# Feed-forward input products of a two-layer decoder trunk: seven half-size products in place of eight, three weight sums by adding transfers, Silu in place of tanh

## The chip, the core and the metric

The kernel runs on one core of a Trainium2 chip. A core has five engines that work side by side, each through a queue of its own in program order: TensorE (PE, with its weight loads shown apart as PEld), VectorE (DVE), ScalarE (ACT), GpSimd (POOL) and SyncE (SP, which here only issues transfers). Sixteen DMA engines move data. The metric is device microseconds of one execution; before the change the median of three runs is 1450.72 us (1449.16 to 1450.77).

## The reference, cut to what matters

512 tokens of width 1024 go through two layers. Each layer has a mixer (attention with a forget gate and a short convolution in layer 0, a gated linear recurrence in layer 1), a cross-attention into 256 memory rows, and a feed-forward block; each of the three adds its normalised output to the residual stream. All data are float32. The change concerns the first half of the feed-forward block:

```python
D_FF = ((8 * D_MODEL // 3 + 255) // 256) * 256          # 2816
def swiglu(h, w_gu, w_down):
    g, u = jnp.split(h @ w_gu, 2, axis=-1)
    return (jax.nn.silu(g) * u) @ w_down
...
        h = rmsnorm(x, g_ffn_pre[layer])
        y = swiglu(h, w_ffn_gu[layer], w_ffn_down[layer])
        x = x + rmsnorm(y, g_ffn_post[layer])
```

`h @ w_gu` is a product of 512x1024 by 1024x5632, twice in the kernel (once a layer).

## The kernel before

**Numbers.** A float32 operand is split into two parts of 12 significant bits, high and low, and a product is high by high plus low by high plus high by low, three matmuls into one float32 sum in PSUM (`mm3`, L276 to L279). So every weight that comes in is split: ACT casts it to the high part (L354, `wh`), DVE subtracts that from the raw value for the low part (L355, `wl`). `split_out` does both.

**Feed-forward, first half** (`ffn`, L634 on). The weights come in chunks of 256 columns and all 1024 rows, as two transfers of 512 KB on SP's queue (`load_raw`, L117) into buffers called `st`, of which there are four; the split parts go into four `wh` and four `wl` buffers. A chunk times the activations `hT` (features on partitions, four row tiles in each half of the features, 512 tokens) gives two blocks of 128 columns by 512 tokens, each in one PSUM bank. That is 2 blocks x 8 row tiles x 3 = 48 matmuls with 512 tokens as the moving side. There are 11 pairs of chunks (jp = 0 to 10), each one gate chunk and one up chunk. jp 0 is special (`ws_gemm_split`, L332): it runs the first 256 tokens and then the other 256, so that the norm of the last tokens can go on beside it. The other 10 pairs are 20 plain chunk products in each layer, 40 in all; the text calls each of them a chunk. Then `act` makes silu(gate) x up from the banks: a tanh on ACT, (tanh + 1) x gate on DVE, times up on DVE, twice the wanted value; the factor of a half is put in when `parts` splits the result for the next product (L657 on).

**What is around it.** Ahead stands the cross-attention's output product (`OutProj.half1`, L418), which for each of four tiles of 128 tokens runs the residual and the next norm (`chain`, `next`; one small power on POOL at L210 for each of the two norms) and the transposes that fill `hT` (`put_T`, L258, with copies out of PSUM by ACT at L268 and DVE at L269). Behind it stands the feed-forward's second product, `OutProj.run` with `w_ffn_down`; its left side is made by `parts`, two row tiles at a time.

**What sets the order.** PE's instructions stand in the order in which the program writes them. The other engines' instructions are put in order by a scheduler when the program is built; on the chip each engine then takes its queue strictly in that order, and an instruction that waits holds up all that stand behind it. A buffer of a pool (`st`, `wh`, `wl`, the 14 large groups, the 8 small `s` tiles, 4 + 4 PSUM banks) is used again as soon as its last reader is done, and the transfer or write that takes it waits for that reader.

Of the kernel before, what the change touches and what calls it, by code (L numbers as in the profile page):

```python
# [15 lines left out]
P = 128  # L16
# [26 lines left out]
def trunk_kernel(ctx: ExitStack, tc: tile.TileContext, a: dict, out: bass.AP):  # L43
    """Residual stream x stays on chip, tokens on partitions. Each sub-layer's input is normalised,
    transposed (features on partitions) and split exactly into two float32r parts of 12 significant
    bits; weights are split the same way. A float32 product is then high*high + low*high + high*low
    in the float32 accumulators of PSUM."""
# [54 lines left out]
    def load_gain(ap, engine=nc.scalar):  # L102
        """A gain spread over the partitions, as two halves of the features."""
# [50 lines left out]
    def log1p(e, w, s):  # L154
        """log(1 + e) for e in [0, 1], as 2 artanh(e / (2 + e)); e is overwritten by the result."""
# [18 lines left out]
    def setup_chan():  # L174
# [8 lines left out]
        # lamc = -8 softplus(-lam), lamh = half of it  # L183
# [16 lines left out]
    def rstd(st):  # L200
        """st[:, 0:2] sums of squares of the halves -> st[:, 4:5] = (mean + eps) ** -0.5"""
# [14 lines left out]
    def row_stats(xt, both=False):  # L216
        """(mean of squares + eps) ** -0.5 of the rows of one tile"""
# [12 lines left out]
    def scaled(xt, g, r):  # L230
        """Both halves of the normalised rows of one tile, tokens on partitions."""
# [13 lines left out]
    class Feat:  # L245
        """Activations with features on partitions: tile k's high and low parts."""
# [4 lines left out]
    def new_hT():  # L251
# [3 lines left out]
        ft.ghi, ft.glo = hi, lo  # L255
        return ft

    def put_T(hT, t, hs, bank=bankB):  # L258
        for hf in range(2):
# [6 lines left out]
            sl = slice(t * P, (t + 1) * P)  # L266
            last = (
# [13 lines left out]
    def w_chunk(w, c0):  # L281
        """256 columns of w, all rows: two pieces of four row tiles."""
# [815 lines left out]
```

## Time and profile before

| What | Before |
|---|---|
| runs | 1449.16, 1450.72, 1450.77 us |
| span of the profiled execution | 1447.4 us, 3.3 us under the median of the runs |
| PE busy, matmuls | 1437.3 us (99%), 7124 |
| DVE busy | 769.6 us (53%) |
| ACT busy | 567.8 us (39%) |
| POOL busy | 37.6 us (3%) |
| transfers | 151.03 MB, 104 GB/s over the span |
| the 20 chunks of layer 0 | from 419.24 us to 636.87 us, 217.6 us |
| the 20 chunks of layer 1 | from 1103.53 us to 1321.16 us, 217.6 us |

A page of the profile has the busy time of each engine, the span in 40 slices, the transfer queues, the chain of work that ended last, and the costliest groups of instructions by line. In a group's row stand the line, engine, operation, out<-in by the program's names and the shape, then busy time, the mean of one in ns, and the idle time of the engine ahead of it with what ended it. Matmuls overlap in the pipeline, so the mean of one matmul is longer than the distance between the starts of two; the distance is what counts and is read from the timeline. The profiled execution is one run; its span leaves out what lies ahead of the first and behind the last instruction.

### The profile page before, as it was taken

The numbers are of one execution on the slowest core, as the hardware profiler recorded it, in microseconds if no ns is written. First come the engines' busy times: TensorE is split into PE (matmuls) and PEld (weight loads), VectorE is DVE, ScalarE is ACT, GpSimd is POOL, SyncE is SP. The second block draws the span as 40 slices with busy tenths as digits, with TensorE's granted clock in tenths as the row PEclk, the third lists the DMA queues.
The fourth block names the chain that finished last, engine by engine and source line by source line (L and its number), as shares of the span: only waits on it lengthen the run. The fifth ranks groups of instructions, "written<-read, shape, count | busy, mean of one in ns | idle before, by whom it ended". The sixth has DMA issues, their size and how long they took to land.

```text
span 1447.4 us, 17847 instructions
## 1 busy us (share of the span) xinstructions
PE 1437.3 (99%) x7124; PEld 1208.5 (83%) x7124; DVE 769.6 (53%) x1171; ACT 567.8 (39%) x922; POOL 37.6 (3%) x82
## 2 busy tenths in 40 slices
PE   8999999999999999999999999999999999999998
PEld 6777789888898888888889888988889888888886
DVE  5785767544743333362447998754484333336232
ACT  4354455433532222252334786443362222225130
POOL 1000001000100000000000000000010000000000
PEclk9999999999999999999999999999999999999999
DMA  5633253520433323323513226352032323323321
GB/s 175 187 95 87 78 174 97 177 80 30 124 97 100 102 89 101 102 88 102 166 46 93 90 88 211 108 162 74 29 117 88 102 88 102 101 88 102 96 79 58
DMA packets 119373, 151.03 MB, mean 104 GB/s; under 512 B 6181, under 2 KB 88177, under 8 KB 119290
## 3 DMA queue, kind: packets, MB, share of 16 engines
q1 hardware_dynamic: 114722, 140.92, 31.3%
q10 hardware_dynamic: 3896, 6.86, 1.7%
q0 software_dynamic: 672, 2.11, 0.5%
q8 instruction: 56, 0.92, 0.3%
q14 instruction: 27, 0.22, 0.1%
HBM read 147.76 MB, written 2.11 MB: 104 GB/s over the span
## 4 chain that ended last, share of the span: by engine, by line
PE 98%; DMA 1%; DVE 0%; issue 0%; POOL 0%; SPq 0%; ACT 0%; DVEq 0%; POOLq 0%; ACTq 0%
PE bA L277 19%; PE bA L279 19%; PE bA L278 19%; PE bA L378 5%; PE bA L380 5%; PE bB L378 5%; PE bB L380 5%; PE bA L379 5%; PE bB L379 5%; PE bA L703 1%; PE bB L262 1%; PE bB L277 1%; PE bA L544 1%; PE bA L546 1%; PE bB L278 1%; PE bB L279 1%
## 5 line engine op out<-in xcount | busy, mean ns | idle before, releaser
L355 DVE TENSOR_TENSOR wl<-st,wh 128x1024 fp32r<-128x1024 f32 x228 | 278.6, 1223 | 402.9 <-ACT wh L354 401.7
L277 PE MATMUL bA<-hTh,wh 128*128 128x512 f32 (+1 forms) x1216 | 456.9, 376 | 0.0
L279 PE MATMUL bA<-hTh,wl 128*128 128x512 f32 (+1 forms) x1216 | 453.2, 373 | 0.0
L278 PE MATMUL bA<-hTl,wh 128*128 128x512 f32 (+1 forms) x1216 | 452.9, 372 | 0.0
L354 ACT CAST wh<-st 128x1024 fp32r<-128x1024 f32 x228 | 239.9, 1052 | 514.0 <-PE bA L278 359.7
L279 PEld LDWEIGHTS bA<-hTh,wl 128*128 128x128 f32 x1216 | 229.0, 188 | 40.3
L278 PEld LDWEIGHTS bA<-hTl,wh 128*128 128x128 f32 x1216 | 229.2, 189 | 38.6
L277 PEld LDWEIGHTS bA<-hTh,wh 128*128 128x128 f32 x1216 | 229.1, 188 | 38.5
L378 PE MATMUL bB<-wh,y 128*128 128x512 f32 x208 | 80.9, 389 | 0.0
L379 PE MATMUL bB<-wl,y 128*128 128x512 f32 x208 | 80.9, 389 | 0.0
L380 PE MATMUL bB<-wh,y 128*128 128x512 f32 x208 | 80.9, 389 | 0.0
L378 PE MATMUL bA<-wh,y 128*128 128x512 f32 x144 | 56.5, 392 | 0.0
L656 DVE TENSOR_TENSOR y<-sw,bA 128x512 f32<-128x512 f32 x44 | 30.2, 686 | 49.5 <-PE bA L279 49.3
L380 PE MATMUL bA<-wh,y 128*128 128x512 f32 x144 | 56.1, 390 | 0.0
L379 PE MATMUL bA<-wl,y 128*128 128x512 f32 x144 | 56.1, 389 | 0.0
L653 DVE SCALAR_TENSOR_TENSOR sw<-sw,bA 128x512 f32<-128x512 f32 x44 | 30.1, 683 | 35.1 <-ACT sw L652 35.1
L380 PEld LDWEIGHTS bB<-wh,y 128*128 128x128 f32 x208 | 39.0, 188 | 8.1
L378 PEld LDWEIGHTS bB<-wh,y 128*128 128x128 f32 x208 | 39.0, 188 | 8.1
L379 PEld LDWEIGHTS bB<-wl,y 128*128 128x128 f32 x208 | 39.0, 188 | 8.1
L652 ACT ACTIVATE sw<-bA 128x512 f32<-128x512 f32 x44 | 26.1, 594 | 48.1 <-PE bA L279 48.1
L210 POOL TENSOR_TENSOR post<-post,nhalf 128x1 f32<-128x1 f32 x24 | 13.2, 548 | 1004.0 <-DVE post L206 1004.0
L236 DVE SCALAR_TENSOR_TENSOR h<-x,pre,gain 128x512 f32<-128x512 f32 x44 | 31.3, 748 | 14.2 <-POOL pre L210 13.5
(248 smaller groups left out, 2035.8 us busy)
## 6 DMA issues: line engine op xcount, KB each, us to landing
st<-in_w_ffn_gu_dram SPq DMA_DIRECT2D x88, 512.0 KB, 3.6
st<-in_w_ffn_down_dram SPq DMA_DIRECT2D x44, 512.0 KB, 3.8
st<-in_w_xkv_dram SPq DMA_DIRECT2D x32, 512.0 KB, 5.0
st<-in_ab_w_in_dram SPq DMA_DIRECT2D x24, 512.0 KB, 3.8
st<-in_w_xq_dram SPq DMA_DIRECT2D x16, 512.0 KB, 3.5
st<-in_w_xo_dram SPq DMA_DIRECT2D x16, 512.0 KB, 3.6
st<-in_c_w_in_dram SPq DMA_DIRECT2D x16, 512.0 KB, 3.9
st<-in_ab_w_out_dram SPq DMA_DIRECT2D x8, 512.0 KB, 3.7
```

The source lines that it names most:

```text
L236: nc.vector.scalar_tensor_tensor(out=h, in0=xt[:, sl], scalar=r, in1=g[hf], op0=ALU.mult, op1=ALU.mult)
L277: nc.tensor.matmul(out=ps, lhsT=wh, rhs=xh, start=first, stop=False)
L278: nc.tensor.matmul(out=ps, lhsT=wh, rhs=xl, start=False, stop=False)
L279: nc.tensor.matmul(out=ps, lhsT=wl, rhs=xh, start=False, stop=last)
L354: nc.scalar.copy(out=hi, in_=src)
L355: nc.vector.tensor_tensor(out=lo, in0=src, in1=f(hi), op=ALU.subtract)
L378: nc.tensor.matmul(out=ps, lhsT=yh, rhs=wh[:, kk, :], start=first, stop=False)
L379: nc.tensor.matmul(out=ps, lhsT=yh, rhs=wl[:, kk, :], start=False, stop=False)
L380: nc.tensor.matmul(out=ps, lhsT=yl, rhs=wh[:, kk, :], start=False, stop=last)
L652: nc.scalar.activation(out=s, in_=gb[m], func=AF.Tanh, scale=0.5)
L653: nc.vector.scalar_tensor_tensor(out=s, in0=s, scalar=1.0, in1=gb[m], op0=ALU.add, op1=ALU.mult)
L656: nc.vector.tensor_tensor(out=y2[jp // 2][:, jp % 2 * 2 + m, :], in0=s, in1=ub[m], op=ALU.mult)
```

## The change

**Activations.** While the transposes of the feed-forward's norm leave PSUM, ACT also copies the unsplit value into two more groups (`hT.raw`, one for each half of the features). Feature halves and token halves (early 256, late 256) make four blocks: a11, a12 (late tokens) and a21, a22 (early tokens). After jp 0, DVE makes four differences of them in place, and each is split into a new group (`wa`).

**Weights.** A chunk's two row halves and two column blocks make B11, B12, B21, B22. The sums that are needed are t1 = B11 + B12, t3 = B12 + B22, t2 = t1 + B22 and t4 = t1 + B21 + B22. A third `st` buffer `tt` is loaded with the upper rows again, and a transfer from POOL's queue with an add at its destination puts the lower rows on top; a second adding transfer puts B11 on top of B12 in `r0`. (In the words of the change these are three sums: two column blocks in the first, one in the second.) DVE then adds `t2` and the first block of `tt`. Four splits follow instead of two: `r0`, `t2` (half as large), `tt` and `r1`.

**Products.** A chunk is now 7 products of 4 row tiles x 3 matmuls with 256 tokens as the moving side, 84 matmuls, in the order a11 b11, s2 t2, n1 t1, n3 t3, a12 b21, a22 t4, n4 b22. Between them ACT copies the first product out of PSUM, and DVE combines the products: three operations of 256 columns (q, u, v) and then two of 256 and one of 512 columns into the result. The gate chunk uses the four banks of one PSUM pool and the up chunk the four of the other.

**Silu.** ACT computes Silu itself, so the DVE operation with (tanh + 1) is gone, and `parts` needs no factor of a half. For chunks jp 1 to 10 Silu and the product with up run on data that the combination has written to SBUF.

The lines that only lost a comment are left out of the diff.

```diff
     def new_hT():
...
-        ft.ghi, ft.glo = hi, lo
+        ft.ghi, ft.glo, ft.raw = hi, lo, None
         return ft
     def put_T(hT, t, hs, bank=bankB):
...
             sl = slice(t * P, (t + 1) * P)
+            if hT.raw:
+                nc.scalar.copy(out=hT.raw[hf][:, :, sl], in_=v)
             last = (
...
+    class Winograd:
+        def __init__(self, hT):
+            r0, r1 = hT.raw
+            e, l = slice(0, 256), slice(256, 512)
+            a21, a11, a22, a12 = r0[:, :, e], r0[:, :, l], r1[:, :, e], r1[:, :, l]
+            sub = lambda o, i0, i1: nc.vector.tensor_tensor(out=o, in0=i0, in1=i1, op=ALU.subtract)
+            self.parts = {}
+            sub(a22, a21, a22)
+            sub(a21, a21, a11)
+            sub(a11, a11, a22)
+            for name, raw in (("s2", a11), ("n1", a22), ("n3", a21)):
+                self.put(name, raw)
+            sub(a12, a12, a11)
+            self.put("n4", a12)
+            for name, hf, sl in (("a11", 0, l), ("a12", 1, l), ("a22", 1, e)):
+                self.parts[name] = hT.ghi[hf][:, :, sl], hT.glo[hf][:, :, sl]
+
+        def put(self, name, raw):
+            g = group("wa")
+            self.parts[name] = g[:, :, 0:256], g[:, :, 256:512]
+            split_out(raw, *self.parts[name])
+
+        def weights(self, w, c0):
+            r0, r1 = load_raw(w, 0, 4, c0, 256), load_raw(w, 4, 4, c0, 256)
+            one, two = slice(0, P), slice(P, 2 * P)
+            add = lambda o, i0, i1: nc.vector.tensor_tensor(out=o, in0=i0, in1=i1, op=ALU.add)
+            t2 = sbuf("t2").rearrange("p (k c) -> p k c", k=4)
+            rows = w.rearrange("(k p) n -> p k n", p=P)
+            tt = load_raw(w, 0, 4, c0, 256)
+            nc.gpsimd.dma_start(out=tt, in_=rows[:, 4:8, c0:c0 + 256], accum_op=ALU.add)
+            nc.gpsimd.dma_start(out=r0[:, :, two], in_=rows[:, 0:4, c0:c0 + P], accum_op=ALU.add)
+            add(t2, tt[:, :, two], r0[:, :, one])
+            add(tt[:, :, one], tt[:, :, one], tt[:, :, two])
+            w1, w2 = split_w(r0, 4, 256), split_w(t2, 4, P)
+            w3, w4 = split_w(tt, 4, 256), split_w(r1, 4, 256)
+            return {"b11": (w1, one), "t1": (w1, two), "t2": (w2, one), "t4": (w3, one),
+                    "t3": (w3, two), "b21": (w4, one), "b22": (w4, two)}
+
+        def gemm(self, w, c0, bank, out):
+            ws = self.weights(w, c0)
+            one, two = slice(0, 256), slice(256, 512)
+            bks = [bank() for _ in range(4)]
+            x, y = sbuf("wx"), sbuf("wy")
+            p1, q, v, u = x[:, one], x[:, two], y[:, one], y[:, two]
+            def product(ps, a, b):
+                (hi, lo), (wt, ms) = self.parts[a], ws[b]
+                for k in range(4):
+                    mm3(ps, wt[0][:, k, ms], wt[1][:, k, ms], hi[:, k, :], lo[:, k, :], k == 0, k == 3)
+                return ps
+            tt = lambda o, i0, i1, op: nc.vector.tensor_tensor(out=o, in0=i0, in1=i1, op=op)
+            ps = product(bks[0][:, one], "a11", "b11")
+            nc.scalar.copy(out=p1, in_=ps)
+            ps = product(bks[1][:, one], "s2", "t2")
+            tt(q, ps, p1, ALU.subtract)
+            ps = product(bks[2][:, one], "n1", "t1")
+            tt(u, ps, q, ALU.add)
+            ps = product(bks[0][:, two], "n3", "t3")
+            tt(v, ps, q, ALU.add)
+            p2 = product(bks[3][:, two], "a12", "b21")
+            p4 = product(bks[3][:, one], "a22", "t4")
+            out(0, slice(256, 512), p2, p1, ALU.add)
+            out(0, slice(0, 256), p4, v, ALU.subtract)
+            product(bks[2][:, two], "n4", "b22")
+            out(1, slice(0, 512), bks[2], y, ALU.add)
...
+        hTf.raw = [f(group("raw")) for _ in range(2)]
         proj.half1()
...
-                nc.scalar.activation(out=s, in_=gb[m], func=AF.Tanh, scale=0.5)
-                nc.vector.scalar_tensor_tensor(
-                    out=s, in0=s, scalar=1.0, in1=gb[m], op0=ALU.add, op1=ALU.mult
-                )
-                nc.vector.tensor_tensor(out=y2[jp // 2][:, jp % 2 * 2 + m, :], in0=s, in1=ub[m], op=ALU.mult)
+                nc.scalar.activation(out=s, in_=gb[m], func=AF.Silu)
+                nc.vector.tensor_tensor(out=y_[:, m, :], in0=s, in1=ub[m], op=ALU.mult)
+        def act_wino(jp, wino):
+            s = [sbuf("sw") for _ in range(2)]
+            def gate(m, sl, ps, sb, op):
+                nc.vector.tensor_tensor(out=s[m][:, sl], in0=ps, in1=sb, op=op)
+                if sl.start == 0:
+                    nc.scalar.activation(out=s[m], in_=s[m], func=AF.Silu)
+            def up(m, sl, ps, sb, op):
+                nc.vector.tensor_tensor(out=y_[:, m, sl], in0=ps, in1=sb, op=op)
+                if sl.start == 0:
+                    nc.vector.tensor_tensor(out=y_[:, m, :], in0=y_[:, m, :], in1=s[m], op=ALU.mult)
+            wino.gemm(w, jp * 256, bankB, gate)
+            y_ = y_rows(jp)
+            wino.gemm(w, FF + jp * 256, bankA, up)
...
-            split_out(src, yg[:, 0:2, :], yg[:, 2:4, :], 0.5)
+            split_out(src, yg[:, 0:2, :], yg[:, 2:4, :])
...
         gb, ub = ws_gemm_split(w, [0, FF], hT, prev.hook)
         act(0, gb, ub)
+        wino = Winograd(hT)
         for jp in range(1, NFF // 2):
-            gb = ws_gemm(w, jp * 256, hT)
-            ub = ws_gemm(w, FF + jp * 256, hT)
-            act(jp, gb, ub)
+            act_wino(jp, wino)
```

The scheduler places the new work as follows. First, DVE's queue in the middle of layer 0's chunks, of the changed kernel, from the end of one up chunk into the next gate chunk. (`bA_4528` is the bank that the last of the seven products fills; `sw` is Silu's result; `st_4632` is the next chunk's `tt`, `st_4627` its `r0`, `st_4629` its `r1`, so that `wl_4643`, `wl_4647` and `wl_4651` are the low parts of `t2`, `tt` and `r1`; `wx_4658` takes q, `st_4754` is the `r0` of the chunk after.)

```order
L749 TENSOR_TENSOR y2_4244<-y2_4244,sw_4371 128x512
L747 TENSOR_TENSOR y2_4244<-bA_4528,wy_4531 128x512
L384 TENSOR_TENSOR t2_4631<-st_4632,st_4627 128x512
L749 TENSOR_TENSOR y2_4244<-y2_4244,sw_4372 128x512
L384 TENSOR_TENSOR st_4632<-st_4632 128x4x128
L432 TENSOR_TENSOR wl_4643<-t2_4631,wh_4642 128x512
L432 TENSOR_TENSOR wl_4647<-st_4632,wh_4646 128x1024
L432 TENSOR_TENSOR wl_4651<-st_4629,wh_4650 128x1024
L412 TENSOR_TENSOR wx_4658<-bB_4655,wx_4658 128x256
L432 TENSOR_TENSOR wl_4766<-st_4754,wh_4765 128x1024
```

Before, at the same place, four splits and four operations on the activations served a pair of chunks:

```order
L355 TENSOR_TENSOR wl_4768<-st_4765,wh_4767 128x1024
L653 SCALAR_TENSOR_TENSOR sw_4757<-sw_4757,bA_4645 128x512
L355 TENSOR_TENSOR wl_4774<-st_4771,wh_4773 128x1024
L653 SCALAR_TENSOR_TENSOR sw_4761<-sw_4761,bA_4646 128x512
L355 TENSOR_TENSOR wl_4830<-st_4827,wh_4829 128x1024
L656 TENSOR_TENSOR y2_4624<-sw_4757,bA_4707 128x512
L656 TENSOR_TENSOR y2_4624<-sw_4761,bA_4708 128x512
```

So the operations that make a chunk's `t2`, `t2`'s low part and `tt`'s low part now stand behind the operation that reads the last product of the chunk before, and q stands behind the splits of `tt` and `r1`.

Second, SP's queue of the changed kernel at the same chunks, with the semaphores that each transfer waits for. (`DMAHW` are raised by SP's and ACT's transfers, `DMASW` by POOL's, `DVE` and `Activation` by those engines; in POOL's queue of the same kernel, below it, the row of `st_4504` raises `DMASW4`, that of `st_4499` `DMASW3`.)

```order
L119 DMA st_4499<-in_w_ffn_gu_dram 128x4x256 [waits DMAHW0_49,DVE_49]
L119 DMA st_4501<-in_w_ffn_gu_dram 128x4x256 [waits DMAHW2_49,DMASW1_49,DMAHW6_49,DVE_49,Activation_49]
L119 DMA st_4504<-in_w_ffn_gu_dram 128x4x256 [waits DMASW2_49,DVE_49]
L119 DMA st_4627<-in_w_ffn_gu_dram 128x4x256 [waits DMAHW3_49,DVE_49]
L119 DMA st_4629<-in_w_ffn_gu_dram 128x4x256 [waits DMAHW1_49,DMASW3_49,DMAHW5_49,DVE_49,Activation_49]
L119 DMA st_4632<-in_w_ffn_gu_dram 128x4x256 [waits DMASW4_49,DVE_49]
```

```order
L389 DMA st_4499<-in_w_ffn_gu_dram 128x4x128
L388 DMA st_4504<-in_w_ffn_gu_dram 128x4x256
L389 DMA st_4627<-in_w_ffn_gu_dram 128x4x128
L388 DMA st_4632<-in_w_ffn_gu_dram 128x4x256
```

Each chunk's `tt` is loaded into the buffer of the `tt` of the chunk before (`st_4632` waits for the add into `st_4504` and for DVE, the last to read it), while `r0` and `r1` turn over the three other buffers. POOL's queue then holds only the adding transfers, `r0`'s ahead of `tt`'s. Before the change POOL had no work here, and SP's transfers waited for DVE's splits alone.

Third, DVE's queue of the changed kernel in the norm ahead of the feed-forward block of layer 0, where the first chunk's `tt` (`st_3869`) is already in hand. (`x1` is the residual of the second tile of tokens, `hTl` the low parts of the first tile's transposes, `pre_3485` the second tile's mean square.)

```order
L526 SCALAR_TENSOR_TENSOR x1_111<-yb_3453,post_3338,x1_111 128x512
L271 TENSOR_TENSOR hTl_2639<-bA_3469,hTh_2637 128x4x128
L384 TENSOR_TENSOR st_3869<-st_3869 128x4x128
L271 TENSOR_TENSOR hTl_2640<-bA_3477,hTh_2638 128x4x128
L202 TENSOR_SCALAR pre_3485<-pre_3485 128x1
```

Before, the two `hTl` operations and the mean square followed each other directly; now an operation that needs the result of the adding transfer stands between them.

More of the change, by code (lines that the diff above doesn't have):

```diff
@@ L549, in memory_kv, with cross @@
         return kh, kl, vh, vl
-    def cross(layer, hT, kv, proj):
+    def cross(layer, hT, kv, proj, hTf):
         kh, kl, vh, vl = kv
@@ L1067, in trunk_kernel @@
         pc = OutProj(a["w_xo"][layer], None, KT, a["g_cross_post"][layer], a["g_ffn_pre"][layer], hTf)
-        cross(layer, hTc, kv, pc)
+        cross(layer, hTc, kv, pc, hTf)
         hT = new_hT() if layer == 0 else None
```

5 lines of the change are left out of this document (4 added, 1 removed).

## The prediction, made blind

> **What bounds the kernel now.** I read first the chain that ended last, then the feed-forward stage by windows, then the starts of single matmuls.
>
> ```profile
> PE 98%; DMA 1%; DVE 0%; issue 0%; POOL 0%; SPq 0%; ACT 0%; DVEq 0%; POOLq 0%; ACTq 0%
> ```
> ```profile
> core 0: us, PE busy (x) PEld busy (x) DVE busy (x) ACT busy (x) POOL busy (x), PEclk, DMA share, GB/s
> 418.50:636.50 218.00, 218.00 (x967) 180.64 (x966) 78.08 (x83) 57.53 (x66) 0.00 (x0) 1.00 0.33 101
> ```
>
> TensorE sets the time from end to end; in layer 0's 20 chunks it never rests, DVE works 78 of 218 us and the DMA engines a third. A saving on PE shows in full if the other engines keep up, and there is no slack behind which a stall of PE could hide. The next rows are PE's timeline: chunks of today, then the memory's key product, which already runs with 256 tokens as the moving side, and the two ends of the chunks.
>
> ```profile
> 499.74 0.39 PE L278 MATMUL bA<-hTl,wh 128*128 128x512 f32 x1
> ...
> 502.91 0.39 PE L277 MATMUL bA<-hTh,wh 128*128 128x512 f32 x1
> ```
> ```profile
> 239.78 0.28 PE L277 MATMUL bA<-mTh,wh 128*128 128x256 f32 x1
> ...
> 242.90 0.28 PE L279 MATMUL bA<-mTh,wl 128*128 128x256 f32 x1
> ```
> ```profile
> 419.24 0.40 PE L277 MATMUL bA<-hTh,wh 128*128 128x512 f32 x1
> ...
> 636.87 0.39 PE L378 MATMUL bB<-wh,y 128*128 128x512 f32 x1
> ```
>
> The first pair is 15 matmuls, so 14 distances in 3.17 us: 0.226 us each. The second pair is 27, 26 distances in 3.12 us: 0.120 us. The third marks a stage of 217.6 us, 10.88 us a chunk.
>
> **PE's own gain.** A chunk goes from 48 matmuls (10.88 us) to 84 x 0.120 = 10.08 us: 0.80 us saved, 32 us over 40 chunks, not the eighth that counting products promises, since a half-wide matmul costs 0.53 of a wide one.
>
> **DVE's queue.** Costs come from these groups (mean ns behind the comma):
>
> ```profile
> L355 DVE TENSOR_TENSOR wl<-st,wh 128x1024 fp32r<-128x1024 f32 x228 | 278.6, 1223 | 402.9 <-ACT wh L354 401.7 <-PE bB L876 0.6
> L656 DVE TENSOR_TENSOR y<-sw,bA 128x512 f32<-128x512 f32 x44 | 30.2, 686 | 49.5 <-PE bA L279 49.3
> L653 DVE SCALAR_TENSOR_TENSOR sw<-sw,bA 128x512 f32<-128x512 f32 x44 | 30.1, 683 | 35.1 <-ACT sw L652 35.1
> L1012 DVE TENSOR_TENSOR q<-q 128x512 f32<-128x512 f32 x8 | 5.2, 688 | 3.0 <-ACT q L1009 3.0
> L355 DVE TENSOR_TENSOR pT<-bB,pT 128x256 fp32r<-128x256 f32 x8 | 3.4, 421 | 1.7 <-ACT pT L354 1.6
> L354 ACT CAST wh<-st 128x1024 fp32r<-128x1024 f32 x228 | 239.9, 1052 | 514.0 <-PE bA L278 359.7 <-PE bB L380 76.2 <-PE bA L380 34.0
> ```
>
> Per chunk DVE gets three large splits (3.67), the split of t2 and two sums (0.69 each), five operations of 256 columns (2.1), one of 512 (0.69), and two products with Silu in every second chunk (0.69 on average): 9.2 us, against 3.9 today. It fits into 10.08, but not in this order. By the queue shown above, the last combination of a chunk, the sum for t2, (after an up chunk) a product with Silu, the sum in tt and the low part of t2 stand in a row. The first can start only when the last product is done, 0.16 us (0.28 less 0.12) after PE may start the next chunk; it and the three others end 0.16 + 4 x 0.69 = 2.91 us after that moment, 3.60 behind an up chunk. PE needs t2's low part at its 15th matmul, 14 x 0.120 = 1.68 us in. So it waits 1.23 or 1.92 us even if every transfer were free. Ten waits of the first kind and nine of the second in a layer: 20 x 10.08 + 12.3 + 17.3 = 231.2 us, 13.6 longer than now. The DVE operation removed by Silu (30 us busy, row L653) was not on PE's chain; I count nothing for it.
>
> **Tables and copies on ACT.** Silu adds a table load in jp 0 of each layer, and the norm's transposes are copied out twice more (8 copies a layer):
>
> ```profile
> L268 ACT CAST hTh<-bB 128x512 fp32r<-128x512 f32 x36 | 19.3, 593 | 38.8 <-PE bB L262 38.7
> L1009 ACT ACT_TABLE_LOAD x4 | 5.1, 1283 | 0.1
> ```
>
> ACT waited 38.7 us for PE ahead of such copies, and the matmuls of the output product and of jp 0 run beside them, so I take nothing; without that cover a layer would pay 8 x 0.59 + 1.28 = 6.0 us.
>
> **The tt buffer.** Each tt is loaded into the buffer of the tt before. That makes a loop in which PE has no part: low part of tt done, load, add, sum for t2, sum in tt, cast, low part. Its transfers:
>
> ```profile
> st<-in_w_ffn_gu_dram SPq DMA_DIRECT2D x88, 512.0 KB, 3.6
> cb<-cum POOLq DMA_DIRECT2D x8, 256.0 KB, 3.7
> cum<-e POOLq DMA_DIRECT2D x1, 16.0 KB, 2.5
> ```
> ```profile
> L835 POOL DMA_DIRECT2D cb<-cum x8 | 4.6, 580 | 79.3 <-DVE fx L857 47.1 <-DVE y L355 21.0 <-PE bB L876 8.8
> ```
> ```profile
> 500.84 1.05 ACT L354 CAST wh<-st 128x1024 fp32r<-128x1024 f32 x1 [3.90 <-PE bA L278]
> 501.93 1.23 DVE L355 TENSOR_TENSOR wl<-st,wh 128x1024 fp32r<-128x1024 f32 x1 [3.62 <-ACT wh L354]
> 503.19 16.69 SPq L119 DMA_DIRECT2D st<-in_w_ffn_gu_dram  x4
> ```
>
> Load 3.6, two sums 1.38, the Silu product every second time 0.34, cast 1.05, low part 1.22, and five hand-overs of 0.04 (ACT's end at 501.89 to DVE's start): 7.8 us, plus A, the time from issue to landing of a 512 KB adding transfer. No transfer here adds, so A is bounded. From below 3.6, a plain load from SP. On POOL's queue 240 KB more cost 1.2 us, so 512 KB would land after 5.0; if the destination is read as a second stream of equal size, after 7.5. Issuing 512 rows rather than 128 might cost four times 0.58: 9.2 at the top. I take 6.3, between one stream and two on that queue. The DMA engines themselves would not be the bound:
>
> ```profile
> q1 hardware_dynamic: 114722, 140.92, 31.3%
> ```
>
> 140.92 MB in 31.3% of 1447.4 us is 311 GB/s when busy; a chunk's three plain loads (1.57 MB) are 5.1 us, its adds (0.79 MB) 2.5 or, read twice, 5.1. The loop is then 14.1 us a chunk (11.4 to 17.0), so it, not PE (10.08) nor DVE's order (11.6 on average), sets the pace, and PE rests about 4 us in each chunk.
>
> [...]
>
> **A layer's stage.** When PE starts the first of the 20 chunks, DVE still owes the second product of jp 0, two splits of activation differences and tt's: about 4.5 us. Then load, hand-over and add: the second tt lands at 14.5. Eighteen loops of 14.1 later (268.3) the last one lands; two sums and t2's low part (2.1) and 70 matmuls (8.4) end the stage at 278.8 us, 61.2 longer than now, 122.4 for both layers.
>
> **The edges.** The two rows below, of POOL, and those of DVE show the norm ahead of the block; the starts are those of the powers for the first tile, and of the last two splits of jp 0.
>
> ```profile
> 379.60 0.55 POOL L210 TENSOR_TENSOR post<-post,nhalf 128x1 f32<-128x1 f32 x1 [141.06 <-DVE post L206]
> 382.84 0.55 POOL L210 TENSOR_TENSOR pre<-pre,nhalf 128x1 f32<-128x1 f32 x1 [2.69 <-DVE pre L206]
> ```
> ```profile
> 376.77 1.23 DVE L355 TENSOR_TENSOR wl<-st,wh 128x1024 fp32r<-128x1024 f32 x1 [0.20 <-ACT wh L354]
> ...
> 386.90 1.28 DVE L269 TENSOR_TENSOR hTl<-bA,hTh 128x512 fp32r<-128x512 f32 x2
> ```
>
> The first tt can be loaded when the split that starts at 376.77 is done (378.0), lands near 381.8 and is added by 388 to 390. DVE's sum in it stands between the two hTl operations that ran at 386.90, and the next norm behind them: 0 to 4 us, I take 2. At the end of the stage, the first low part of y waits for the last combination (0.16 + 0.69 + 1.22 after the last product) and PE wants it 0.45 us in: 1.7 us. Both layers: 7.4.
>
> **The sum.** 1447.4 + 122.4 + 7.4 = 1577.2 us of span; the span is 3.3 under the median of the runs, so **1580.5 us**.
>
> **Rivals.**
>
> - *The destination's read counts in full, or more.* A = 7.5, loop 15.3: second tt at 15.7, last at 291.1, end at 301.6, 84 a layer: 1626 us. With A = 9.2 it is 1690. For it: two operands have to come from somewhere. Against: nothing here shows that the reads can't overlap.
> - *Transfers hide, DVE's order decides.* If an add lands as fast as SP's loads, the loop (11.4) falls under DVE's 11.6: 1447.4 + 27.2 + 7.4 + 3.3 = 1485 us. Against it: POOL's queue took 3.7 us for half the bytes.
> - *Faster.* If the loop and DVE's row both stay under PE's 10.08 us a chunk, 32 us are gained against 7 at the edges: 1426 us. The point from which it decides is an A below 2.3 together with t2's low part within 1.68 us; DVE's four operations in a row alone need 2.91.
> - *PE's clock falls in its rests.* The windows of the start, where PE paused, show it:
>
> ```profile
> 8.00:12.00 4.00, 3.01 (x13) 1.90 (x12) 2.81 (x5) 2.94 (x4) 0.00 (x0) 0.78 1.04 406
> 12.00:14.00 2.00, 2.00 (x7) 1.57 (x6) 1.73 (x5) 1.68 (x4) 0.80 (x1) 0.59 1.04 399
> 14.00:16.00 2.00, 1.53 (x9) 0.98 (x8) 1.55 (x3) 0.00 (x0) 0.67 (x1) 1.00 1.02 265
> ```
>
>   About 3.4 us of half clock (0.44 of 4, 0.82 of 2). One such spell a chunk adds 1.7 us to PE's 10.08 and stays hidden under 14.1. Only if the mean clock fell below 10.08 / 14.1 = 0.71 would PE decide; at half clock throughout a chunk is 20.2 us, 185.6 more a layer: 1829 us.
>   [...]
>
> **How the numbers follow.** Forecast (A between 5 and 7) 0.50; a slower add (1626 to 1690) 0.23; DVE's order alone 0.13; half clock 0.05; faster 0.07; gain and edges cancel, no change, 0.02. A measurement here tells about 0.2% from nothing. So faster 0.07, same 0.02, slower 0.91. The range runs from DVE's order alone, with a little less at the edges, 1480, to the top of A, 1690; it leaves out both ends of the clock and the faster case. The forecast's own range, A from 5 to 7, is 1532 to 1608 (38 us for each us of A: 19 additions in each of two layers).
>
> **What would show each step.** Matmuls at L279 to L281 with 256 tokens 0.120 us apart; PE busy well under 99% in the stage, with pauses at each chunk's second product; the sum for t2 (L384) waiting for `tt`'s adding transfer and not for PE; SP's load of tt waiting for DVE; chunks about 14 us apart; issue to landing of the 512 KB add near 6.3. If the sum for t2 starts right behind the combination, DVE's order decides and I mis-sized A; if PE never waits in mid-chunk, the order has more slack than I gave it; if PEclk falls under 0.7 in the stage, the clock decides.

## The result and the profile after

The changed kernel takes 1598.13 us (median of 4 runs, 1595.20 to 1598.68) against 1449.94 us (1448.89 to 1450.77): a ratio of 1.102, 95% interval 1.100 to 1.103. It is 10% slower; 1580.5 us had been predicted, in a range of 1480 to 1690. The profiled execution has a span of 1596.7 us, 149.3 us more than before (1447.4). First the page, its row of PE and its transfer queues:

```profile
PE 1475.8 (92%) x8564; PEld 1303.5 (82%) x8564; DVE 980.6 (61%) x1543; ACT 661.0 (41%) x1069; POOL 139.5 (9%) x162
...
q1 hardware_dynamic: 135842, 161.90, 32.3%
q0 software_dynamic: 42912, 33.58, 14.7%
...
PE 12%; DMA 11%; DVE 4%; ACT 1%; issue 1%; POOL 0%; POOLq 0%; DVEq 0%; ACTq 0%
```

PE, which had 98% of the chain of waits before, is now one link among others (the shares add up to 29%: the chain is followed back only to some 1134 us), and the adding transfers on POOL's queue (q0) take 14.7% of the DMA engines for 33.58 MB. Where the time went is read from the ends of the two stages, PE's timeline:

```profile
424.57 0.28 PE L279 MATMUL bB<-hTh,wh 128*128 128x256 f32 x1
...
711.89 0.50 PE L455 MATMUL bB<-wh,y 128*128 128x512 f32 x1 [0.53 <-ACT y L431]
...
1184.59 0.28 PE L279 MATMUL bB<-hTh,wh 128*128 128x256 f32 x1
...
1469.37 0.50 PE L455 MATMUL bB<-wh,y 128*128 128x512 f32 x1 [0.53 <-ACT y L431]
```

The stages take 287.3 and 284.8 us (217.6 each before): 69.7 and 67.2 us more. Layer 0's starts 5.3 us later (419.24 before). Between the stages lie 472.7 us (466.7 before), 6.0 us more; behind the second one 1.1 us more. Together 149.3. So 137 us are lost inside the chunks and 12 us around them. The windows over the two stages:

```profile
core 0: us, PE busy (x) PEld busy (x) DVE busy (x) ACT busy (x) POOL busy (x), PEclk, DMA share, GB/s
424.57:711.89 287.32, 236.24 (x1683) 227.90 (x1681) 174.83 (x261) 92.19 (x123) 47.08 (x37) 0.89 0.74 163
1184.59:1469.37 284.78, 234.50 (x1683) 226.29 (x1681) 174.50 (x261) 92.12 (x123) 47.14 (x37) 0.90 0.73 163
```

In the first stage no engine is full: PE is busy 82%, DVE 61%, the DMA engines 74%. A loop of waits looks like that. The waits of PE, of DVE and of SP's queue (us in total, times, longest) name its members:

```profile
PE bA L279 <- ACT wh L431: 49.5, 20, 4.1
PE bB L279 <- ACT wh L431: 38.2, 18, 4.2
```
```profile
DVE t L384 <- DMA st<-in_w_ffn_gu_dram: 59.2, 35, 3.4
```
```profile
SPq L119 <- DVE wl L432: 815.2, 171, 40.9
```

In 38 of 40 chunks PE stops some 2.3 us for the high part of a weight (at the second product, t2's); in 35 of 40 the sum for t2 (L384) waits for a transfer and not for PE; and SP's loads wait for DVE's low parts. The chain of waits in one chunk of layer 1, in order of time (start, duration, what), goes once round:

```profile
1272.48 1.24 DVE wl L432
...
1273.74 3.57 DMA st<-in_w_ffn_gu_dram
...
1277.37 0.49 issue
1277.87 5.93 DMA st<-in_w_ffn_gu_dram
...
1283.82 0.70 DVE t L384
...
1284.60 0.55 ACT wh L431
1285.15 0.34 ACT wx L414
1285.49 0.95 ACT wh L431
...
1286.47 1.24 DVE wl L432
```

Low part of tt, load of the next tt, add, sum for t2, casts, low part of the next tt: 13.99 us, and PE appears nowhere. (The three ACT rows are the cast of t2, the copy of the first product and the cast of tt.) Over 18 chunks of each layer the sums for t2 are 14.45 and 14.38 us apart.

### The profile page after: what moved, and what is told of

Read it like the earlier page. It is cut to its first block, busy times and chain, and to the rows that moved or that the text cites. A ratio compares the mean times of both kernels' runs of the same rounds, so it can differ in the third digit from the quotient of the medians.

```text
span 1596.7 us, 21725 instructions
## 1 busy us (share of the span) xinstructions
PE 1475.8 (92%) x8564; PEld 1303.5 (82%) x8564; DVE 980.6 (61%) x1543; ACT 661.0 (41%) x1069; POOL 139.5 (9%) x162
## 3 DMA queue, kind: packets, MB, share of 16 engines
q1 hardware_dynamic: 135842, 161.90, 32.3%
q0 software_dynamic: 42912, 33.58, 14.7%
## 5 line engine op out<-in xcount | busy, mean ns | idle before, releaser
L279 PE MATMUL bA<-hTh,wh 128*128 128x256 f32 (+1 forms) x816 | 276.1, 338 | 0.0
L281 PE MATMUL bA<-hTh,wl 128*128 128x256 f32 (+1 forms) x816 | 272.4, 334 | 0.0
L280 PE MATMUL bA<-hTl,wh 128*128 128x256 f32 (+1 forms) x816 | 272.1, 333 | 0.0
L281 PEld LDWEIGHTS bA<-hTh,wl 128*128 128x128 f32 x816 | 155.0, 190 | 15.4
L279 PEld LDWEIGHTS bA<-hTh,wh 128*128 128x128 f32 x816 | 155.2, 190 | 13.5
L279 PE MATMUL bA<-wa,wh 128*128 128x256 f32 x320 | 105.2, 329 | 49.5 <-ACT wh L431 49.5
L279 PE MATMUL bB<-wa,wh 128*128 128x256 f32 x320 | 102.2, 319 | 38.2 <-ACT wh L431 38.2
L279 PEld LDWEIGHTS bA<-wa,wh 128*128 128x128 f32 x320 | 74.4, 232 | 53.5 <-ACT wh L431 53.5
L281 PE MATMUL bB<-wa,wl 128*128 128x256 f32 x320 | 102.5, 320 | 9.7 <-DVE wl L432 9.7
L281 PE MATMUL bA<-wa,wl 128*128 128x256 f32 x320 | 105.3, 329 | 2.9 <-DVE wl L432 2.9
L280 PE MATMUL bA<-wa,wh 128*128 128x256 f32 x320 | 102.3, 320 | 0.0
L280 PE MATMUL bB<-wa,wh 128*128 128x256 f32 x320 | 100.0, 313 | 0.0
L744 ACT ACTIVATE sw<-sw 128x512 f32<-128x512 f32 x40 | 25.3, 632 | 137.6 <-DVE sw L742 137.6
```

The lines of the kernel that those rows point to most:

```text
L279: nc.tensor.matmul(out=ps, lhsT=wh, rhs=xh, start=first, stop=False)
L280: nc.tensor.matmul(out=ps, lhsT=wh, rhs=xl, start=False, stop=False)
L281: nc.tensor.matmul(out=ps, lhsT=wl, rhs=xh, start=False, stop=last)
L744: nc.scalar.activation(out=s[m], in_=s[m], func=AF.Silu)
```

## The experiments

Line numbers differ from kernel to kernel. Names in the rows: `t` is t2, `st` a buffer of r0 or r1, `tt` the buffer of tt where it has a pool of its own. "Chunk" is the mean distance of the sums for t2 over 18 chunks in layer 0 and layer 1.

### The add alone: plain transfers in its place

```diff
-            nc.gpsimd.dma_start(out=tt, in_=rows[:, 4:8, c0:c0 + 256], accum_op=ALU.add)
-            nc.gpsimd.dma_start(out=r0[:, :, two], in_=rows[:, 0:4, c0:c0 + P], accum_op=ALU.add)
+            nc.gpsimd.dma_start(out=tt, in_=rows[:, 4:8, c0:c0 + 256])
+            nc.gpsimd.dma_start(out=r0[:, :, two], in_=rows[:, 0:4, c0:c0 + P])
```

> The changed kernel with the adding transfers turned into plain ones: same queue, size, rows, waits and order, but the destination is overwritten instead of added to (so each weight sum lacks one summand and the products are not the wanted ones). This prices the add itself. If an add is dear because the destination is read as a second stream, the 512 KB transfer lands about 1.7 to 2 us earlier (3.9 to 4.2 us instead of 5.9), the loop falls from 14.4 to 12.5 us a chunk and the time to about 1530 us; the queue's share of the DMA engines falls from 14.7% to about 7.5% at the plain rate of 314 GB/s. Rival, the cost is POOL's issue of 512 rows and its queue: landing still at 5.5 to 6 us, time 1585 to 1598 us.

Measured: 1541.0 us, ratio 1.063 (1.061 to 1.065), chunk 13.09 and 12.89 us. Every queue has the same order as in the change. The issue rows of POOL's transfers (KB, median us from issue to landing) of the change:

```profile
st<-in_w_ffn_gu_dram POOLq DMA_DIRECT2D x40, 512.0 KB, 5.9
...
st<-in_w_ffn_gu_dram POOLq DMA_DIRECT2D x40, 256.0 KB, 5.2
```

and, with the queue's row, of the plain kernel:

```profile
q0 software_dynamic: 9632, 33.58, 7.1%
...
st<-in_w_ffn_gu_dram POOLq DMA_DIRECT2D x40, 512.0 KB, 4.1
...
st<-in_w_ffn_gu_dram POOLq DMA_DIRECT2D x40, 256.0 KB, 3.5
```

The loop falls by 1.4 us, to 13.1 and 12.9, a little less than expected (12.5, 1530 us). So the add costs 1.8 us of landing time, 57 us of the whole kernel, and twice the time on the DMA engines: 14.7% of 1596.7 us is 235 us or 143 GB/s, 7.1% of 1543.8 us is 110 us or 306 GB/s for the same bytes. The rival (queue and issue alone) falls. Two things differ at once, though: an add is made, and the bytes travel in 42,912 packets instead of 9,632. The size of the packets does not explain the time on the DMA engines. In the last kernel of "One add less, then the edges", between 500 and 600 us, both queues move packets of 1 KB (packets, MB, share of 16 engines):

```profile
q1 hardware_dynamic: 15465, 15.36, 45.7%
q0 software_dynamic: 5280, 5.24, 35.4%
```

The plain loads of q1 go at 15.36 MB in 45.7 us, 336 GB/s, the adds of q0 at 5.24 MB in 35.4 us, 148 GB/s. So the factor of two belongs to the add. What in an add takes that time no row shows; the second stream, a read of the destination, was the author's assumption.

### No adding transfers

```diff
-            nc.gpsimd.dma_start(out=tt, ... accum_op=ALU.add)
-            nc.gpsimd.dma_start(out=r0[:, :, two], ... accum_op=ALU.add)
```

> The two adding transfers of a chunk are left out and everything else stays (so the weight sums t1 to t4 lack a summand and the products are not the wanted ones; the number of operations on the engines is the same). Loop theory: the loop loses the add's 5.9 us, 14.4 - 5.9 = 8.5 us, and DVE's order sets 11.2 to 11.6 us a chunk; the front edges lose their 2 to 3 us a layer too: about 1598 - 108 - 5 = 1485 us. Rival, DVE's order alone bounds the chunk: no change, near 1595 us. If it comes out near the time with a second tt buffer, the adds' load on the DMA engines costs nothing beside their place in the loop; if it is clearly faster, that load matters.

Measured (the sum in tt is kept behind the sum for t2, as in the change): 1449.41 us, ratio 1.000 (0.999 to 1.001); stages 216.2 us, a chunk every 10.8 us. PE's waits in the whole run:

```profile
PE bA L279 <- ACT wh L430: 13.0, 20, 0.7
PE bA L281 <- DVE wl L431: 4.5, 20, 0.2
```

It is 149 us faster than the change: everything that the change loses comes with the adds. It is also 36 us faster than expected, because DVE's order cost less. PE waits 0.65 and 0.23 us behind each gate chunk; with the slower restarts around the two waits the distances between matmuls add up to 1.4 us there (1.23 had been predicted). Behind an up chunk PE waits for nothing: there the scheduler put the sum for t2 and its low part ahead of the last combination. So 20 x 10.08 + 10 x 1.4 = 215.6 us, as measured within 1 us.

### A second tt buffer; the order; both

Second buffer (kept in all runs below whose rows name `tt`):

```diff
-WS = 4
+WS = 3                      # r0 and r1
+    wtt = ctx.enter_context(tc.tile_pool(name="wtt", bufs=2))
-            tt = load_raw(w, 0, 4, c0, 256)
+            with tc.issue_after(marks[0]):          # behind r1's load on SP
+                tt = load_raw(w, 0, 4, c0, 256, wtt, "tt")
+            with tc.issue_after(t2i.ins):           # sum in tt behind sum for t2
```

Order: the weights of the next chunk become steps between this chunk's products.

```diff
             ps = product(bks[2][:, one], "n1", "t1")
             tt(u, ps, q, ALU.add)
+            next(nxt)            # r0's split, sum for t2, t2's split, sum in tt
...
             p4 = product(bks[3][:, one], "a22", "t4")
+            next(nxt)            # tt's split
...
             product(bks[2][:, two], "n4", "b22")
+            self.ws = next(nxt)  # r1's split
```

> The buffer tt gets a second copy (r0 and r1 turn over three buffers as before; the gains' pool gives up two buffers for the room; the sum in tt stays queued behind the sum for t2). Loop theory: the 14.4 us from one tt to the next now cover two chunks, so the loop falls to 7.2 us a chunk and the next limit shows: DVE's order, 11.2 to 11.6 us a chunk, or the DMA engines, 10.9 us a chunk (0.147 of 1596.7 us, 235 us, of adding transfers over 40 chunks, and 1.57 MB at 314 GB/s). Some 36 loops by 3.0 us: 1598 - 108 = 1490 us. Rival, adding transfers are slow whatever waits for them (they run one after the other, or the DMA engines are full): no change, 1590 to 1600 us. Rival, DVE's order was the bound all along: no change either, but then the sum for t2 starts right behind the combination instead of waiting for the transfer.

> The order alone: the next chunk's sums and splits are issued between this chunk's products (r0 and t2 behind the third, tt behind the sixth, r1 behind the seventh), with one tt buffer as in the change. Loop theory: tt's load still waits for tt's own split, so the loop stays, at 13.8 to 14.4 us a chunk (it may lose the product with Silu, 0.3 us on average, out of the row): 1575 to 1598 us. Rival, DVE's order is what makes PE wait: 10.1 to 10.9 us a chunk, 1440 to 1475 us.

> Second tt buffer and the order together. Loop theory: neither the loop (7.2 us) nor DVE's row is left; PE needs 10.08 us a chunk, DVE 9.2 us, the DMA engines 10.9 us if an add takes 2.2 times the time per byte of a plain load: 10.1 to 10.9 us a chunk, stage 202 to 218 us, with edges of 5 us a layer 1430 to 1465 us. If PE is the bound, near 1430; if the DMA engines are, near 1465, with their share close to 1 in the stage. Rival, a further wait that the loop hid: above 1480 us.

Measured: second buffer 1561.3 us (ratio 1.078, 1.076 to 1.079; chunk 13.59 and 13.86), order alone 1590.6 us (1.098, 1.096 to 1.099; chunk 14.14 and 14.21), both 1545.3 us (1.066, 1.065 to 1.068; chunk 13.25 and 13.50). The order alone came out as the loop theory said. The second buffer did not: 108 us were expected and 37 came. Both together missed too, by 80 us (1430 to 1465 expected); their rival, a further wait that the loop hid, is what came out. The rows of the run with both, of DVE, SP and POOL, show why:

```profile
564.38 0.69 DVE L388 TENSOR_TENSOR t<-tt,st 128x512 f32<-128x512 f32 x1 [4.47 <-DMA tt<-in_w_ffn_gu_dram]
...
577.26 0.69 DVE L388 TENSOR_TENSOR t<-tt,st 128x512 f32<-128x512 f32 x1 [4.79 <-DMA tt<-in_w_ffn_gu_dram]
```
```profile
556.94 8.58 SPq L122 DMA_DIRECT2D st<-in_w_ffn_gu_dram  x2
565.57 0.50 SPq L122 DMA_DIRECT2D tt<-in_w_ffn_gu_dram  x1
```
```profile
570.80 1.28 POOL L393 DMA_DIRECT2D tt<-in_w_ffn_gu_dram  x1 [8.39 <-DMA tt<-in_w_ffn_gu_dram]
```

The first row of SP is two loads, r0's at 556.94 and r1's 8.58 us later at its end. tt's load has its buffer free, but stands in SP's queue behind r1's, which goes into the buffer of the r0 before and so waits for the last reader of that r0: the sum for t2, at 564.38. Then 1.2 us to tt's issue, 5.2 to the add's, 6.5 to its landing: 12.9 us. A loop of the same kind, closed through another buffer and a queue.

### tt's load ahead of r1's

```diff
+            r0 = load_raw(w, 0, 4, c0, 256)
+            with tc.issue_after(marks[0]):
+                tt = load_raw(w, 0, 4, c0, 256, wtt, "tt")
+            with tc.issue_after(marks[0]):
+                r1 = load_raw(w, 4, 4, c0, 256)
```

> Second tt buffer, sums and splits between the products (as in the run before), and now tt's load issued ahead of r1's. New theory: with r1 ahead, tt's load stood in SP's queue behind a load that waits for r0's buffer, that is for the sum for t2, which waits for the adding transfer: sum 0.7, load 4.7, add 6.6, two issues and hand-overs 1.1, together 13.1 us a chunk as measured. With tt ahead this loop covers two chunks (7.8 us a chunk with the splits) and the next limit shows: the DMA engines, 5.9 us of adds and 5.0 us of plain loads, 10.9 us a chunk, about 1470 us; or, if they have more to give, PE at 10.08 us a chunk, about 1430 us. Rival: an add is slow for another reason (its queue takes one at a time, POOL issues late), and the chunk stays near 13 us: 1540 us.

> The same buffers and SP order, but DVE's order as the scheduler makes it in the change (the last combination, the sum in tt and the product with Silu ahead of t2's low part). This prices DVE's order where no loop hides it: predicted were 1.23 us behind a gate chunk and 1.92 us behind an up chunk, about 30 us a layer, 60 us in all above the run with the order written out, if PE bounds that one (1490 us against 1430); if the DMA engines bound both, the two come out within 15 us of each other. The run without adding transfers showed PE waits of 0.65 and 0.23 us behind a gate chunk only, since the scheduler had another order there.

Measured: 1459.6 us, ratio 1.007 (1.005 to 1.009), chunk 11.06 and 11.05 us; with the scheduler's own DVE order 1474.3 us in its one run, chunk 10.99 and 11.35 us. The window 500 to 600 us of the first and its DMA queues in it (packets, MB, share of 16 engines):

```profile
core 0: us, PE busy (x) PEld busy (x) DVE busy (x) ACT busy (x) POOL busy (x), PEclk, DMA share, GB/s
500.00:600.00 100.00, 97.75 (x795) 95.66 (x794) 76.75 (x120) 41.23 (x55) 23.14 (x19) 1.00 0.97 216
```
```profile
q0 software_dynamic: 10020, 7.37, 54.1%
q1 hardware_dynamic: 14256, 14.16, 42.7%
```

One line of order brings 86 us. Now the DMA engines are most likely the bound: in this window they are 97% busy (91% over the stage) although they deliver only 216 GB/s, with more than half of their time spent on a third of the bytes, and the 10.9 us a chunk worked out from the change's queues is met. The run below with a third of the adding bytes gone bears it out, although it also spares r0 the wait for its add. DVE's order costs at most about 15 us here (one run), and behind an up chunk the scheduler had again put the sum for t2 ahead of the last combination.

### ACT copies tt's upper rows

```diff
-                tt = load_raw(w, 0, 4, c0, 256, wtt, "tt")
+            tt = wtt.tile([P, 4, 256], F32, tag="tt", name="tt")
+            nc.scalar.copy(out=tt, in_=r0)
+            with tc.issue_after(powers[0]):         # adds behind the norm's last power
```

> As the run with tt's load ahead, but tt's upper rows are copied by ACT from r0 (1.05 us a chunk on ACT) instead of being loaded a second time, and the adding transfers of a layer stand in POOL's queue behind the norm's last power, the first sum in DVE's queue behind the norm's last transposes. If the DMA engines bound the chunk, their 10.9 us fall by 0.52 MB at 314 GB/s, 1.7 us, to 9.2 us, under PE's 10.08: 1425 to 1435 us, faster than before the change. If PE bounds it already, only the edges gain: some 5 us under the run with tt's load ahead. Rival: ACT's copy comes late in its queue behind casts that wait, the add starts later, and the time is above 1445 us.

Measured: 1512.3 us, ratio 1.044 (1.042 to 1.046), chunk 12.46 us. A miss: the DMA engines are down to 73% and the chunk is longer. Rows of ACT and POOL:

```profile
559.21 1.05 ACT L397 COPY tt<-st 128x1024 f32<-128x1024 f32 x1 [0.37 <-DMA st<-in_w_ffn_gu_dram]
...
569.81 1.05 ACT L457 CAST wh<-st 128x1024 fp32r<-128x1024 f32 x1 [3.92 <-DMA st<-in_w_ffn_gu_dram]
571.20 1.04 ACT L397 COPY tt<-st 128x1024 f32<-128x1024 f32 x1 [0.34 <-DMA st<-in_w_ffn_gu_dram]
```
```profile
560.55 1.26 POOL L399 DMA_DIRECT2D tt<-in_w_ffn_gu_dram  x1 [9.19 <-ACT tt L397]
561.30 1.82 POOL L400 DMA_DIRECT2D st<-in_w_ffn_gu_dram  x1
```

Both adds of a chunk now start when the copy is done, r0's behind tt's; it lands 8.5 us after its issue, the cast of r0 at 569.81 waits for it, and the next copy stands behind that cast on ACT: 12.0 us from copy to copy. The rival written down beforehand (the copy late behind casts that wait) is what happened.

### One add less, then the edges

```diff
-            nc.gpsimd.dma_start(out=r0[:, :, two], ... accum_op=ALU.add)
+            add(r0[:, :, two], r0[:, :, two], r0[:, :, one])
```

> As the run with tt's load ahead (11.06 us a chunk, 1459.6 us), but the second sum (B11 on B12 in r0) is made by DVE (0.60 us a chunk) instead of a 256 KB adding transfer. Theory: there the DMA engines were full (54.1 + 42.7% of the time in its stage). Without a third of the adding bytes they need about 1.9 us a chunk less, 9.1 us, DVE has 9.8 us of work, and PE sets the pace with 10.08 us: about 10.2 us a chunk, 1425 to 1435 us, faster than before the change by 1%. Rival, DVE becomes the bound, since its queue waits at each sum: 10.6 us a chunk or more, 1445 us and above.

> As the run beside it, and the edges mended: a layer's first adding transfers stand in POOL's queue behind the norm's last power, the first sum for t2 behind the norm's last transposes on DVE, and outside the chunks the loads go round all five buffers (three st and two tt), so that the last load of jp 0 need not wait. The norm ahead of the block cost 5.3 us in layer 0 and the stretch between the stages 6.0 us with the change, against 0.4 and 1.3 us without adding transfers: expected are 5 to 10 us less than the run beside it, 1418 to 1428 us if that one comes out near 1430. Rival, what delays the norm is ACT's extra copies and not POOL's queue: no difference.

Measured: 1435.19 us, ratio 0.990 (0.989 to 0.992), chunk 10.10 and 10.14 us, and with the edges mended 1424.74 us, ratio 0.983 (0.982 to 0.985). Both are a little faster than the kernel before, by 1.0% and 1.7%. The stage of layer 0 in the second (columns as in the window above):

```profile
420.06:622.61 202.55, 201.97 (x1683) 201.66 (x1681) 179.04 (x279) 94.53 (x123) 22.87 (x18) 1.00 0.80 206
```

PE hardly rests; 20 x 10.08 = 201.6 us was PE's own need. This is the gain that the change meant to bring, and DVE, 88% busy, just follows. With 204.4 us in layer 1 the two stages are 28.4 us shorter than before, and 4.0 us are lost around them.

### The edges alone, in the changed kernel

```diff
+            with tc.issue_after(powers[0]):         # POOL: behind the norm's last power
+                ... both adding transfers
+            with tc.issue_after(lows[0]):           # DVE: behind the norm's last low part
+                t2i = add(t2, tt[:, :, two], r0[:, :, one])
+            with tc.issue_after(t2i.ins):
+                add(tt[:, :, one], tt[:, :, one], tt[:, :, two])
```

> The changed kernel with its edges mended and nothing else meant: a layer's first adding transfers stand in POOL's queue behind the norm's last power, the first sum for t2 behind the norm's last transposes on DVE, and the sum in tt behind the sum for t2. Theory: with the change, POOL's powers and DVE's low parts stood behind adding transfers, which cost 5.3 us ahead of layer 0's stage and 4.7 us more between the stages than without adding transfers (472.7 against 468.0 us); without that, the stage of layer 0 starts near 420 us instead of 424.6, the stretch between the stages takes 468 to 470 us, and the time is 1588 to 1591 us, 7 to 10 us less than the change. Rival: ACT's extra copies of the unsplit values are what delays the norm: no difference, 1596 to 1599 us.

Measured: 1586.95 us (5 runs, 1584.4 to 1591.8), ratio 1.096 (1.094 to 1.098), 11 us under the change. The stage of layer 0 starts at 419.94 us and 468.2 us lie between the stages, 4.6 and 4.5 us less than in the change; the rival of ACT's copies, which are still there, falls. The run moves POOL's adds and DVE's sums together, so what delayed the norm in the change is told by its rows, of POOL and of DVE:

```profile
382.94 1.34 POOL L389 DMA_DIRECT2D st<-in_w_ffn_gu_dram  x1 [143.06 <-DMA st<-in_w_ffn_gu_dram]
383.80 1.08 POOL L210 TENSOR_TENSOR post<-post,nhalf 128x1 f32<-128x1 f32 x1
```
```profile
384.91 0.75 DVE L526 SCALAR_TENSOR_TENSOR x<-ya,post,x 128x512 f32<-128x512 f32 x1 [4.41 <-POOL post L210]
...
392.06 0.68 DVE L384 TENSOR_TENSOR st<-st 128x512 f32<-128x512 f32 x1
```

### Silu alone

```diff
-                nc.scalar.activation(out=s, in_=gb[m], func=AF.Tanh, scale=0.5)
-                nc.vector.scalar_tensor_tensor(
-                    out=s, in0=s, scalar=1.0, in1=gb[m], op0=ALU.add, op1=ALU.mult
-                )
+                nc.scalar.activation(out=s, in_=gb[m], func=AF.Silu)
```

> Silu alone: the eight plain products of before, with ACT's Silu in place of tanh and of DVE's operation with (tanh + 1), and no factor of a half in the split. Theory: DVE's operation was not on PE's chain, and the table load for Silu stands beside products: no change, 1447 to 1452 us. Rival: the table load or a longer wait for ACT stalls PE at the two stage starts: 2 to 4 us more.

Measured: 1449.37 us, ratio 1.000 (0.999 to 1.001), with 28 us less work on DVE (741.7 against 769.6). Silu neither gains nor costs.

## Why the prediction was right, and where its terms were off

- **PE's gain.** Predicted 10.08 us a chunk, 201.6 a stage. The two versions with one add less, in which PE hardly waits, have stages of 202.3 and 202.6 us in layer 0, 203.8 and 204.4 in layer 1. Right; in the change itself the gain lies unused under the loop.
- **The tt loop.** Predicted 7.8 + A with A = 6.3, 14.1 us; measured 14.45 and 14.38. The mechanism is the one named, shown by its chain and by taking its members away one by one (add, buffer, queue order). In the chunk shown, of 14.0 us, the load of 3.6 was 3.57, A of 6.3 was 5.93 and the rest 4.5: 0.49 us pass between tt's landing and the start of the add's transfer, where a hand-over of 0.04 had been counted. The mean chunk is 0.4 us longer. Half of that is the product with Silu: behind an up chunk the sum for t2 and the end of tt's low part lie 4.3 us apart, behind a gate chunk 3.9. The other half is loads and adds that land late (an add up to 7.3). Averaged, the rest was 4.7 instead of 4.2 and A 6.0 instead of 6.3. The two errors partly cancel, so that the chunk came out within 0.35 us is in part luck. 0.35 and 0.28 us over 18 loops are 11.3 us of the error.
- **A's bounds.** 3.6 to 9.2 held it. The plain transfer on the same queue landed after 4.1, not the 5.0 taken for one stream, and the add's surcharge was 1.8 us, not the 2.5 of a second stream in full. The A of 6.3 had been 5.0 and half of that surcharge, 1.3: the first term was 0.9 too long and the second 0.5 too short, so A came out only 0.4 under 6.3, which is luck too. The 7.5 of two full streams, an estimate, was too long for the landing, which took 5.9; on the DMA engines the factor of two is there (143 against 306 GB/s).
- **The stage's start and end.** The second sum for t2 starts 14.4 us after PE's first chunk; its transfer was predicted to land at 14.5. What is left of the stages beside the 18 loops is 27.3 and 26.0 us, of which 0.7 belong to the tail: 26.6 and 25.3, against 25.0 (14.5 + 2.1 + 8.4), 1.9 us of the error. The tail was predicted at 1.7 us a layer. The first matmul on y starts 0.81 us behind the last of the products, 0.7 more than the 0.12 between two products, and then PE waits for the low part of y as forecast, which makes the 1.1 us behind each stage:

```profile
713.28 0.50 PE L457 MATMUL bB<-wh,y 128*128 128x512 f32 x1 [0.66 <-DVE y L432]
```

- **DVE's order.** Predicted 1.23 us behind a gate chunk; the distances gave 1.4 where no loop hid it. The 1.92 us behind an up chunk were not measured in the change's own order, since the scheduler reordered there once adds or buffers changed. The rival's price (1485 us) is thus not confirmed, and without adds the kernel took 1449 us.
- **The edges: the step that failed.** 2 us a layer were taken for the norm, put down to DVE's sum in tt between two low parts; it was 5.3 in layer 0 and 4.9 in layer 1 (the 6.0 between the stages without the 1.1 of layer 0's tail). The row at 392.06 shows that this sum waited for nothing. It was POOL: r0's adding transfer stood in its queue ahead of the norm's power and waited there for its data, and DVE waited 4.41 us for that power. The prediction listed POOL's powers and not what stood ahead of them. This is 6.2 us of the error; with the loops' 11.3 and the stages' 1.9 that makes the 19.5 us by which the span was missed, within 0.1. In the time of the runs 1.9 us of it disappear, since the profiled execution lay closer to the median than before the change.
- **The clock.** Predicted one spell of half clock a chunk, hidden. PE's row where t2's high part came late, and the window behind it:

```profile
569.57 0.58 PE L279 MATMUL bB<-wa,wh 128*128 128x256 f32 x1 [4.03 <-ACT wh L431]
```
```profile
569.50:575.00 5.50, 5.12 (x22) 4.83 (x23) 4.74 (x6) 3.33 (x5) 0.00 (x0) 0.50 0.56 166
```

  A rest of 4 us, then 5.3 us at half clock with matmuls 0.21 us apart. The mean of 0.89 in layer 0's stage costs at most 0.11 x 287.3 = 31.6 us, 1.6 us a chunk (1.7 predicted): 11.7 us, under the loop's 14.4. Shorter rests are followed by half clock too. PE rests for 1.6 us from 466.85 us on, and soon after comes this:

```profile
469.21:472.62 3.41, 3.41 (x16) 3.41 (x17) 2.77 (x4) 2.38 (x3) 0.00 (x0) 0.50 0.57 173
```

  The trace has 27 spells of half clock in the 40 chunks, of 3.4 or 6.8 us, and 15 of them begin in or soon after a rest under 3 us; what sets one off is not shown. Where the rests are gone, in the stage of layer 0 with one add less and the edges mended, the clock is 1.00.
- **Silu and its table.** Counted as nothing, and nothing it is: the table load in jp 0 of each layer lasts 1.28 us in the change, and Silu alone has a ratio of 1.000.

## What to carry to other kernels

Before trading PE work for transfers and vector work, walk once round every buffer that is written, read and written again, and through the queues that its transfers stand in: here the longest such loop set the pace, 14.4 us against PE's 10.08, while no engine was more than 82% busy in the stages. Breaking the loop at its buffer was not enough while the next load stood in SP's queue behind one that waited for the same event: 13.25 and 13.50 us a chunk, and 11.06 and 11.05 with that load ahead. An adding transfer took the DMA engines about twice the time of a plain one here (143 against 306 GB/s) and is to be counted so, and an instruction that waits for data must not be queued on POOL ahead of a step that others wait for: it cost DVE a wait of 4.41 us.

## What the runs showed of the hardware that was not expected

- An adding transfer of 512 rows took POOL 1.28 us at its issue, a plain one of the same shape 0.75. The rows (duration in ns, least, median, most) of the change and of the kernel with plain transfers:

```profile
L388 POOL DMA_DIRECT2D st<-in_w_ffn_gu_dram x40: 1268/1277/1302, 385.6 to 1451.7; - x40
```
```profile
L388 POOL DMA_DIRECT2D st<-in_w_ffn_gu_dram x40: 751/751/787, 386.6 to 1400.1; - x40
```
- DVE operations that follow each other without a wait start closer together than they last: in the change the mean of 128x512 is 0.69 us, the starts below are 0.61 apart. The sum of such means overstates the busy queue by a seventh:

```profile
1283.82 0.69 DVE L384 TENSOR_TENSOR t<-st 128x512 f32<-128x512 f32 x1 [2.46 <-DMA st<-in_w_ffn_gu_dram]
1284.43 0.68 DVE L384 TENSOR_TENSOR st<-st 128x512 f32<-128x512 f32 x1
```
- With adding transfers among their work the 16 DMA engines were 97% busy at 216 GB/s (tt's load ahead of r1's, 500 to 600 us), while SP's plain loads in the change went at 314 GB/s of busy time (161.90 MB in 32.3% of the span): it was the share of busy time, not the GB/s, that told when they were full.
